# Second scores product of each head on its own 64 rows of the array, in a parallel mixer layer on one core

## The chip, the cores and the metric

The kernel runs on one core of a Trainium2 chip. The metric is the time of one execution on the device in microseconds (us). Three runs of the kernel before took 1723.13, 1725.75 and 1727.35 us; their median is 1725.75 us. The profile comes from one more execution, which took 1721.93 us, 1720.2 us of it from its first to its last instruction.

## The reference

One layer over 4096 tokens of width 1024. A projection `x @ w_in` gives the inputs of five groups of heads and a gate; the groups' outputs times `silu(gate)` go through `w_out`, and a residual with layer norm follows. The change is in the fifth group, cross-attention of each token to a memory of 256 rows, with four heads of width 64:

```
def memory_cross_attention(q, mem, w_kv):
    k, v = jnp.split(mem @ w_kv, 2, axis=-1)
    q = q.reshape(bn, s, N_SUB, HEAD_DIM)
    k = k.reshape(bn, -1, N_SUB, HEAD_DIM)
    v = v.reshape(bn, -1, N_SUB, HEAD_DIM)
    scores = jnp.einsum("bshd,bmhd->bhsm", q, k) * (1.0 / math.sqrt(HEAD_DIM))
    p = jax.nn.softmax(scores, axis=-1)
    return jnp.einsum("bhsm,bmhd->bshd", p, v).reshape(bn, s, D_G)
```

## The kernel before, in words

The tokens are worked on in four pairs of blocks of 512 (`p`). The big projection is done in 14 pairs of 128 output columns (`mpair`), by a Strassen scheme with seven products each, and every product is made of matrix products of rounded float32 parts (type float32r, one pass of TensorE), a high and a low part for both sides. These are lines L220, L222 and L223, 128 by 128 weights against 512 columns. The output projection at the end is L812.

`attention(p, i, n, src, g)` handles heads `2i` and `2i+1` (called `j` = 0 and 1) for one block of 512 tokens; it is called 16 times. `queries` makes a tile `q` of 128 rows for each head. For head 0 the rows 0 to 63 hold the rounded query and the rows 64 to 127 what the rounding left; for head 1 the halves are exchanged. The keys stand in two tiles. `k1` holds the rounded key on both halves. `k2` holds what the rounding left of the key, on the half where the rounded query stands, and zeros on the other half. So the scores of a head are two products of 128 rows each: `q` by `k1` (`r` = 0) and, on top in the same PSUM bank, `q` by `k2` (`r` = 1). In the second one 64 of the 128 rows are zeros.

Each call does this in two steps (`c2`) of two chunks of 128 tokens (`c`). In a step each head has one PSUM bank, `sc[j]`, with 256 columns for each chunk. A maximum (L622), an exponential (L626), and a division follow on VectorE and ScalarE; transposes (L639) turn the result, and L645 makes the output product. That one has weights of 64 columns only and writes the two heads to different halves of the PSUM partitions; L648 makes the two heads' products follow each other. The mixing in another group (L588) also has weights of 64 columns.

The program is written in the order of the loops, but what stands in each engine's queue is set at build time by a scheduler: it fills TensorE's queue with whatever is ready, so products of the projection, transposes and scores of an attention are mixed. All PSUM banks that are not of the projection come from one pool of four (`pa`, tag `ax`). A matrix product in the trace has two parts, the load of its weights (PEld) and the product (PE). 256 scores products are issued, 128 with `r` = 0 and 128 with `r` = 1.

Of the kernel before, what the change touches and what calls it, by code (L numbers as in the profile page):

```python
# [18 lines left out]
P = 128  # L19
# [33 lines left out]
def trunk(ctx, tc, a, out):  # L53
    nc = tc.nc
# [10 lines left out]
    def nm(s):  # L65
        uid[0] += 1
        return f"{s}_{uid[0]}"
# [5 lines left out]
    def tt(tag, dt=F32, n=None):  # L73
        cols, bufs = SLOTS[tag]
        return (wp if tag == "ws" else tp).tile([P, cols], dt, tag=tag, name=nm(n or tag), bufs=bufs)

    def const(shape, src=None, dt=F32):
        t = cp.tile(shape, dt, name=nm("c"), tag=nm("ct"))
        if src is not None:
            nc.sync.dma_start(out=t, in_=src)  # L80
        return t

    def bank(pool, tag):
        return pool.tile([P, T], F32, tag=tag, name=nm(tag))
# [151 lines left out]
    def mpair(xs):  # L236


        def step(ps, x, start, stop):
            ready(1)  # L240
            product(ps, ahead.pop(0), x, start, stop)
            ready(5)

        A = bank(pm, "mm")
        step(A, xs[PA], True, False)
        t = tt("st", n="t")
        nc.scalar.copy(out=t, in_=A)  # L247
        C = bank(pm, "mm")
        step(C, xs[PT1], True, True)
        B = bank(pm, "mm")  # L250
        step(B, xs[PT2], True, True)
        add(t, B, t)
        v = tt("st", n="v")
        add(v, C, t)
        step(A, xs[PB], False, True)
        B2 = bank(pm, "mm")
        step(B2, xs[PT3], True, False)
        c22 = tt("cc", n="cc")
        add(c22, B2, v)
        C2 = bank(pm, "mm")  # L260
        step(C2, xs[PD], True, True)
        c12 = tt("cc", n="cc")
        add(c12, C2, v)
        step(B2, xs[PT4], False, True)
        c21 = tt("cc", n="cc")
        add(c21, B2, t)
        return (A, c12), (c21, c22)
# [76 lines left out]
    k1, k2 = ([const([P, 2, 256], dt=F32R) for _ in range(2)] for _ in range(2))  # L344
# [73 lines left out]
    def store(b, k, y):  # L418
        nc.sync.dma_start(out=h[b][:, :, k], in_=y.rearrange("p (u t) -> p u t", u=2))
# [179 lines left out]
    def queries(src):  # L599

        q = tt("big", F32R, n="q")[:, :2 * T].rearrange("p (j t) -> p j t", j=2)
        for j in range(2):
            d0, d1 = 64 * j, 64 - 64 * j
            nc.scalar.copy(out=q[d0:d0 + 64, j], in_=src[d0:d0 + 64])
            nc.vector.tensor_tensor(out=q[d1:d1 + 64, j], in0=src[d0:d0 + 64], in1=q[d0:d0 + 64, j].bitcast(F32),
                                    op=ALU.subtract)
        return q

    def attention(p, i, n, src, g):
        q = queries(src)  # L610
        es = [tt("big", n="e")[:, :2 * T].rearrange("p (c m) -> p c m", c=NC4) for _ in range(2)]
        for c2 in range(2):
            sc = [bank(pa, "ax").rearrange("p (c m) -> p c m", c=2) for _ in range(2)]
            for c in range(2):
                t0 = (2 * c2 + c) * P
                for j in range(2):
                    for r, k in enumerate((k1, k2)):
                        nc.tensor.matmul(out=sc[j][:, c], lhsT=q[:, j, t0:t0 + P], rhs=k[i][:, j],  # L618
                                         start=(r == 0), stop=(r == 1))
            for j in range(2):  # L620
                mx = sp.tile([P, 2], F32, tag="mx", name=nm("mx"))
                nc.vector.tensor_reduce(out=mx, in_=sc[j], axis=AX.X, op=ALU.max, negate=True)  # L622
                e = es[j][:, 2 * c2:2 * c2 + 2]
                su = sp.tile([P, 2], F32, tag="su", name=nm("su"))
                for c in range(2):
                    nc.scalar.activation(out=e[:, c], in_=sc[j][:, c], func=AF.Exp, bias=mx[:, c:c + 1],  # L626
                                         accum_out=su[:, c:c + 1])
                ri = sp.tile([P, 2], F32, tag="ri", name=nm("ri"))
                nc.vector.reciprocal(out=ri, in_=su)
                for c in range(2):  # L630
                    nc.vector.tensor_scalar(out=e[:, c], in0=e[:, c], scalar1=ri[:, c:c + 1], scalar2=None,
                                            op0=ALU.mult)
        po = bank(pa, "ax")
        for mc in range(2):
            pTs, copies = [], []
            for j in range(2):
                pt = bank(pa, "ax")
                for c in range(NC4):
                    nc.tensor.transpose(out=pt[:, P * c:P * c + P], in_=es[j][:, c, P * mc:P * mc + P],  # L639
                                        identity=ident)  # L640
                pTs.append(tt("wk", n="pT")[:, :T])
                copies.append(nc.scalar.copy(out=pTs[j], in_=pt))  # L642
            for j in range(2):
                hd = 2 * i + j
                mm = nc.tensor.matmul(out=po[64 * j:64 * j + 64], lhsT=vm[:, mc, 64 * hd:64 * hd + 64], rhs=pTs[j],  # L645
                                      start=(mc == 0), stop=(mc == 1))
                if j == 0:
                    tc.add_manual_dep(mm.ins, copies[1].ins.name,  # L648
                                      mybir.DependencyInfo(mybir.DependencyClass.Sync, mybir.DependencyReason.DATA),
                                      reason="both heads' products follow each other")  # L650
        nc.vector.tensor_tensor(out=g, in0=po, in1=g, op=ALU.mult)
        store(2 * p + n, 8 + i, g)
# [66 lines left out]
    for p in range(NPAIR):  # L719
# [15 lines left out]
        for i in range(2):  # L735
            q, ge = mpair(xs)
            for n in range(2):
                attention(p, i, n, q[n], silu2(ge[n], ge[n]))
            mixing(p, i, vns, *mpair(xs))
# [49 lines left out]
    for b in range(NB):  # L789
        for c in range(NC4):  # L790
# [9 lines left out]
            r = [tt("cc", n="r") for _ in range(2)]  # L800
# [7 lines left out]
            for n, k in steps:  # L808
                hi, lo = hh[k]
                whi, wlo = wo[k]  # L810
                for l, ww in ((lo, whi), (hi, wlo), (hi, whi)):
                    nc.tensor.matmul(out=ps[n], lhsT=l[:, P * (c % 2):P * (c % 2) + P], rhs=ww[:, T * n:T * n + T],  # L812
                                     start=(k == 0 and l is lo), stop=(k == NKO - 1 and ww is whi and l is hi))
# [73 lines left out]
```

## Time and profile before

| what | value |
|---|---|
| median of three runs | 1725.75 us |
| profiled execution | 1721.93 us, span 1720.2 us |
| TensorE busy | 1695.2 us, 99% of the span |
| VectorE busy | 1330.6 us, 77% |
| ScalarE busy | 510.1 us, 30% |
| granted TensorE clock, mean | 0.998 |
| scores products, L618 | 256 |
| output products of attention, L645 | 128 |

A record of TensorE lasts from when a product begins to when its last result has arrived, so records of neighbours overlap. What a product costs the engine is the distance from its start to the start of the next one. In the forms "128*128 128x256" the first pair is the rows and columns of the array that the weights fill, the second the partitions and columns of the operand.

### The profile page before, as it was taken

The page shows a single profiled execution, that of the slowest core. Times are in us where ns is not written, and L with a number is a line of the kernel's source. Part 1 is how long each engine was busy: PE and PEld are TensorE (multiplying, and loading weights), DVE is VectorE, ACT ScalarE, POOL GpSimd, SP SyncE. Part 2 cuts the span into 40 slices and gives each one's busy share as a digit, 9 for nine tenths or more (in the row PEclk, how much of TensorE's full clock was granted, in tenths as well). Part 3 has the DMA queues.
Part 4 walks back from the last instruction along what each step waited for, and adds up shares of the span by engine and source line. Part 5 has one row for each costly group of instructions (what it writes and reads, how often), then busy time and mean ns, then how long its engine had stood idle before and what let it go on. Part 6 is the DMA issues. An engine that isn't in the chain of part 4 may idle for free.

```text
span 1720.2 us, 21845 instructions
## 1 busy us (share of the span) xinstructions
PE 1695.2 (99%) x7924; PEld 1370.5 (80%) x7924; DVE 1330.6 (77%) x2462; ACT 510.1 (30%) x945; POOL 50.0 (3%) x87
## 2 busy tenths in 40 slices
PE   7999999999999999999999999999999999999997
PEld 6887777878877788887778888777888888888786
DVE  8688977899966559997663999775399997555764
ACT  5334654411154332013542311354250101001200
POOL 0000000000100000010000001000000000000000
PEclk9999999999999999999999999999999999999999
DMA  8778455876744577674447767534683334332621
GB/s 278 249 310 317 184 215 224 302 243 206 236 159 147 159 258 256 210 241 163 155 138 265 247 203 230 197 130 157 222 300 123 123 119 158 119 114 74 208 76 48
DMA packets 128379, 333.83 MB, mean 194 GB/s; under 512 B 14096, under 2 KB 36112, under 8 KB 128272
## 3 DMA queue, kind: packets, MB, share of 16 engines
q1 hardware_dynamic: 128272, 332.44, 56.8%
q8 instruction: 63, 1.03, 0.2%
q14 instruction: 44, 0.36, 0.1%
HBM read 239.07 MB, written 93.32 MB: 193 GB/s over the span
## 4 chain that ended last, share of the span: by engine, by line
PE 90%; DVE 5%; DMA 2%; ACT 2%; issue 1%; SPq 0%; DVEq 0%; ACTq 0%
PE mm L812 24%; PE mm L220 19%; PE mm L223 19%; PE mm L222 19%; PE ax L645 2%; PE ax L618 2%; PE ax L639 2%; DVE xl L88 1%; DMA wq<-in_w_in 1%; PE ax L588 1%; DVE xraw L94 1%; PE ax L439 1%; ACT e L626 1%; PE ax L496 1%; PE ax L486 0%
## 5 line engine op out<-in xcount | busy, mean ns | idle before, releaser
L220 PE MATMUL mm<-xl,w 128*128 128x512 f32 x1572 | 619.1, 394 | 10.2 <-DVE xl L88 7.8
L223 PE MATMUL mm<-xh,w 128*128 128x512 f32 x1572 | 617.8, 393 | 0.0
L222 PE MATMUL mm<-xh,w 128*128 128x512 f32 x1572 | 617.6, 393 | 0.0
L812 PE MATMUL mm<-wo,h 128*128 128x512 f32 x1920 | 438.3, 390 | 1.2 <-DVE h L88 1.2
L812 PEld LDWEIGHTS mm<-wo,h 128*128 128x128 f32 x1920 | 360.0, 188 | 76.0 <-DVE h L88 1.7
L220 PEld LDWEIGHTS mm<-xl,w 128*128 128x128 f32 x1572 | 295.8, 188 | 72.0 <-DVE xl L88 7.8
L223 PEld LDWEIGHTS mm<-xh,w 128*128 128x128 f32 x1572 | 295.8, 188 | 63.8 <-issue 3.2
L222 PEld LDWEIGHTS mm<-xh,w 128*128 128x128 f32 x1572 | 296.0, 188 | 60.0 <-issue 1.0
L473 DVE SCALAR_TENSOR_TENSOR acc<-din,c,acc 128x1024 f32<-128x1024 f32 x240 | 304.2, 1280 | 0.3
L87 ACT CAST h<-hraw 128x1024 fp32r<-128x1024 f32 (+1 forms) x48 | 43.4, 911 | 309.7 <-PE mm L812 241.0
L91 DVE TENSOR_TENSOR cc<-mm,v 128x512 f32<-128x512 f32 x110 | 75.4, 688 | 58.8 <-PE mm L223 57.9
L815 DVE SCALAR_TENSOR_TENSOR r<-r,mm 128x512 f32<-128x512 f32 x64 | 43.2, 687 | 73.5 <-PE mm L812 72.2
L247 ACT COPY t<-mm 128x512 f32<-128x512 f32 x55 | 32.3, 587 | 188.0 <-PE mm L223 177.6
L399 ACT ACTIVATE cc<-cc 128x512 f32<-128x512 f32 x44 | 27.8, 633 | 154.1 <-DVE cc L91 154.0
L88 DVE TENSOR_TENSOR xl<-xraw,xh 128x1024 fp32r<-128x1024 f32 x58 | 69.0, 1222 | 5.6 <-ACT xh L87 5.5
L91 DVE TENSOR_TENSOR t<-mm,t 128x512 f32<-128x512 f32 x55 | 37.9, 689 | 44.0 <-PE mm L223 43.3
L87 ACT CAST xh<-xraw 128x1024 fp32r<-128x1024 f32 x58 | 59.2, 1050 | 42.7 <-DVE xraw L94 21.3
L88 DVE TENSOR_TENSOR h<-hraw,h 128x1024 fp32r<-128x1024 f32 (+1 forms) x48 | 49.9, 1041 | 21.8 <-ACT h L87 12.8
L626 ACT ACTIVATE e<-ax,mx 128x256 f32<-128x256 f32 x128 | 59.2, 474 | 14.1 <-DVE mx L622 13.0
L622 DVE TENSOR_REDUCE mx<-ax 128x2 f32<-128x512 f32 x64 | 42.9, 682 | 24.7 <-PE ax L618 24.4
L91 DVE TENSOR_TENSOR cc<-mm,t 128x512 f32<-128x512 f32 x55 | 37.9, 688 | 27.2 <-PE mm L223 27.0
L642 ACT COPY pT<-ax 128x512 f32<-128x512 f32 x64 | 36.1, 589 | 48.1 <-PE ax L639 47.4
(148 smaller groups left out, 1515.7 us busy)
## 6 DMA issues: line engine op xcount, KB each, us to landing
w<-wd SPq DMA_DIRECT2D x294, 512.0 KB, 4.2
wd<-w SPq DMA_DIRECT2D x98, 512.0 KB, 3.2
xraw<-in_xT SPq DMA_DIRECT2D x32, 512.0 KB, 5.0
h<-cc SPq DMA_DIRECT2D x64, 256.0 KB, 3.3
hraw<-h SPq DMA_DIRECT2D x32, 512.0 KB, 4.2
r<-in_x SPq DMA_DIRECT2D x64, 256.0 KB, 3.1
out<-r SPq DMA_DIRECT2D x64, 256.0 KB, 2.0
wraw<-in_w_in SPq DMA_DIRECT2D x24, 512.0 KB, 4.6
```

Source lines behind the costliest of these rows:

```text
L87: nc.scalar.copy(out=hi, in_=src)
L88: nc.vector.tensor_tensor(out=lo, in0=src, in1=hi.bitcast(F32), op=ALU.subtract)
L91: nc.vector.tensor_tensor(out=dst, in0=x, in1=y, op=ALU.add)
L220: nc.tensor.matmul(out=ps, lhsT=w[:, 0, k], rhs=xl[:, r], start=start and k == 0, stop=False, skip_group_check=True)
L222: nc.tensor.matmul(out=ps, lhsT=w[:, 1, k], rhs=xh[:, r], start=False, stop=False, skip_group_check=True)
L223: nc.tensor.matmul(out=ps, lhsT=w[:, 0, k], rhs=xh[:, r], start=False, stop=stop and k == 3, skip_group_check=True)
L473: nc.vector.scalar_tensor_tensor(out=accs[i], in0=dins[i][:, k:k + 2 * T], scalar=dww[:, i, k:k + 1], in1=accs[i], op0=ALU.mult, op1=ALU.add)
L622: nc.vector.tensor_reduce(out=mx, in_=sc[j], axis=AX.X, op=ALU.max, negate=True)
L626: nc.scalar.activation(out=e[:, c], in_=sc[j][:, c], func=AF.Exp, bias=mx[:, c:c + 1], accum_out=su[:, c:c + 1])
L642: copies.append(nc.scalar.copy(out=pTs[j], in_=pt))
L812: nc.tensor.matmul(out=ps[n], lhsT=l[:, P * (c % 2):P * (c % 2) + P], rhs=ww[:, T * n:T * n + T], start=(k == 0 and l is lo), stop=(k == N ...
L815: nc.vector.scalar_tensor_tensor(out=r[n], in0=r[n], scalar=ALPHA, in1=ps[n], op0=ALU.mult, op1=ALU.add)
```

## The change

The loop over `r` moves to the outside: a step first issues the four products with `k1`, of both chunks and both heads, and then the four with `k2`. The products with `k2` take only the 64 rows on which `k2` is not zero, rows 0 to 63 for head 0 and 64 to 127 for head 1. Only the first product into a bank carries the start flag. The number of matrix products and of weight loads stays 256, and each has as many columns as before. Lines behind the loop move down by one (L618 becomes L619, L645 becomes L646).

```
-            for c in range(2):
-                t0 = (2 * c2 + c) * P
-                for j in range(2):
-                    for r, k in enumerate((k1, k2)):
-                        nc.tensor.matmul(out=sc[j][:, c], lhsT=q[:, j, t0:t0 + P], rhs=k[i][:, j],
-                                         start=(r == 0), stop=(r == 1))
+            for r in range(2):
+                for c in range(2):
+                    t0 = (2 * c2 + c) * P
+                    for j in range(2):
+                        d = slice(64 * j, 64 * j + 64) if r else slice(0, P)
+                        nc.tensor.matmul(out=sc[j][:, c], lhsT=q[d, j, t0:t0 + P], rhs=(k1, k2)[r][i][d, j],
+                                         start=(r == c == 0), stop=(r == 1), skip_group_check=True)
```

How TensorE's queue changes is seen at two places. The names are those of the tiles: `c_246` and `c_247` are `k1`, `c_248` and `c_249` are `k2`, each `ax` is the PSUM bank of one head in one step.

First step of the first attention, one bank, before:

```order
L220 MATMUL mm_2051<-xl_257,w_1767 128x512
L618 MATMUL ax_1859<-c_246,q_1852 128x256
L618 MATMUL ax_1859<-c_248,q_1852 128x256
L618 MATMUL ax_1859<-c_246,q_1852 128x256
L618 MATMUL ax_1859<-c_248,q_1852 128x256
L222 MATMUL mm_2051<-xh_256,w_1767 128x512
```

The same place in the changed program:

```order
L220 MATMUL mm_2051<-xl_257,w_1767 128x512
L619 MATMUL ax_1859<-c_246,q_1852 128x256 x2
L619 MATMUL ax_1859<-c_248,q_1852 128x256 x2
L222 MATMUL mm_2051<-xh_256,w_1767 128x512
```

Here the scheduler issues one head's bank alone, so both products with `k2` are of the same head and on the same rows, and a projection product follows.

An attention of the second pair of blocks, around its output products, before (`ax_5237` and `ax_5238` are the two heads of one step, `ax_5265` is a head of the next step):

```order
L618 MATMUL ax_5237<-c_247,q_5230 128x256
L618 MATMUL ax_5237<-c_249,q_5230 128x256
L645 MATMUL ax_5192<-pT_5214,c_250 64x512
L645 MATMUL ax_5192<-pT_5221,c_250 64x512
L618 MATMUL ax_5238<-c_247,q_5230 128x256
L618 MATMUL ax_5238<-c_249,q_5230 128x256
L618 MATMUL ax_5265<-c_247,q_5230 128x256
L618 MATMUL ax_5265<-c_249,q_5230 128x256
L618 MATMUL ax_5265<-c_247,q_5230 128x256
L618 MATMUL ax_5265<-c_249,q_5230 128x256
```

The same place in the changed program:

```order
L619 MATMUL ax_5237<-c_247,q_5230 128x256 x2
L619 MATMUL ax_5238<-c_247,q_5230 128x256 x2
L619 MATMUL ax_5237<-c_249,q_5230 128x256
L619 MATMUL ax_5238<-c_249,q_5230 128x256
L646 MATMUL ax_5192<-pT_5214,c_250 64x512
L646 MATMUL ax_5192<-pT_5221,c_250 64x512
L619 MATMUL ax_5237<-c_249,q_5230 128x256
L619 MATMUL ax_5238<-c_249,q_5230 128x256
L619 MATMUL ax_5265<-c_247,q_5230 128x256 x2
L619 MATMUL ax_5265<-c_249,q_5230 128x256 x2
```

Here two pairs of different heads stand next to each other, one ahead of the output products and one behind them, and the next step's bank has its two of one head again.

## Rows read from the trace of the kernel before

**Rows 1.** Span and granted clock of the core.

```profile
core 0: 1720.2 us, clock 0.998
```

**Rows 2.** The page: busy time, share of the span, instructions; chain that ended last.

```profile
PE 1695.2 (99%) x7924; PEld 1370.5 (80%) x7924; DVE 1330.6 (77%) x2462; ACT 510.1 (30%) x945; POOL 50.0 (3%) x87
PE 90%; DVE 5%; DMA 2%; ACT 2%; issue 1%; SPq 0%; DVEq 0%; ACTq 0%
```

**Rows 3.** Busy time by stretch, here the four that hold the attentions.

```profile
185.00:280.00 95.00, 94.90 (x512) 71.50 (x511) 79.03 (x159) 57.58 (x140) 0.26 (x1) 1.00 0.50 189
505.00:590.00 85.00, 84.72 (x466) 63.72 (x466) 53.57 (x125) 43.59 (x114) 0.21 (x1) 1.00 0.45 149
815.00:900.00 85.00, 84.82 (x467) 63.89 (x466) 53.76 (x126) 43.57 (x114) 0.21 (x1) 1.00 0.44 148
1125.00:1210.00 85.00, 84.80 (x466) 63.83 (x466) 53.67 (x122) 43.58 (x115) 0.21 (x1) 1.00 0.44 147
```

**Rows 4.** Timeline of PE: start, us, engine line op, form, count; one full scores block.

```profile
242.03 0.39 PE L222 MATMUL mm<-xh,w 128*128 128x512 f32 x1
242.26 0.39 PE L223 MATMUL mm<-xh,w 128*128 128x512 f32 x1
242.49 2.08 PE L618 MATMUL ax<-c,q 128*128 128x256 f32 x16
244.40 0.40 PE L220 MATMUL mm<-xl,w 128*128 128x512 f32 x1
```

**Rows 5.** Timeline of PE around one block of L588, weights of 64 columns.

```profile
220.88 0.39 PE L222 MATMUL mm<-xh,w 128*128 128x512 f32 x1
221.10 0.39 PE L223 MATMUL mm<-xh,w 128*128 128x512 f32 x1
221.42 1.97 PE L588 MATMUL ax<-c,nrm 128*64 128x128 f32 x32
223.32 0.50 PE L220 MATMUL mm<-xl,w 128*128 128x512 f32 x1
223.66 0.40 PE L222 MATMUL mm<-xh,w 128*128 128x512 f32 x1
223.89 0.39 PE L223 MATMUL mm<-xh,w 128*128 128x512 f32 x1
```

**Rows 6.** Transposes of whole 128 by 128 tiles, timeline of PE.

```profile
214.38 1.09 PE L639 MATMUL ax<-c,e 128*128 128x128 f32 x8
215.23 0.48 PE L220 MATMUL mm<-xl,w 128*128 128x512 f32 x1
```

**Rows 7.** PE around one block of L645; its lines 2, 3: without earlier starts.

```profile
204.07 0.28 PE L618 MATMUL ax<-c,q 128*128 128x256 f32 x1
204.28 1.08 PE L645 MATMUL ax<-pT,c 128*64 128x512 f32 x4
204.28 1.07 PE L645 MATMUL ax<-pT,c 128*64 128x512 f32 x3
204.76 0.60 PE L645 MATMUL ax<-pT,c 128*64 128x512 f32 x2
205.29 0.74 PE L618 MATMUL ax<-c,q 128*128 128x256 f32 x4
205.87 0.39 PE L222 MATMUL mm<-xh,w 128*128 128x512 f32 x1
```

**Rows 8.** The block of rows 5 again, from its last two products.

```profile
223.11 0.28 PE L588 MATMUL ax<-c,nrm 128*64 128x128 f32 x2
```

**Rows 9.** Weight loads by line: duration min/median/max in ns.

```profile
L618 PEld LDWEIGHTS ax<-c,q x256: 186/189/193, 190.2 to 1187.7; 128*128 128x128 f32 x128
L645 PEld LDWEIGHTS ax<-pT,c x128: 132/134/137, 201.0 to 1197.5; 128*64 128x64 f32 x128
```

**Rows 10.** What PE's weight loads waited for, total us, times, longest.

```profile
PEld ax L645 <- ACT pT L642: 9.0, 24, 0.5
```

## The prediction

> **What bounds the kernel now.** I began with the clock, then the page, then a table by stage, then single starts on TensorE. The clock is whole nearly everywhere [rows 1], so durations are those of the higher level, 2.4 GHz. TensorE is busy for 99% of the span and makes 90% of the chain that ended last [rows 2]. That share is an average, so the four stretches with the attentions matter: TensorE is busy for 94.9 of 95.0 us in the first and about 84.8 of 85.0 in each of the others, VectorE, the next, for 79.0 and about 54 [rows 3]. There TensorE is the bound, and time that its queue gains or loses reaches the end nearly in full. The busy figure is swollen by overlapping records, so I count starts. A block of 16 scores products begins at 242.49 and the next product at 244.40: 1.91 / 16 = 0.119 us each. A projection product with 512 columns takes 0.23, from 242.26 to 242.49 [rows 4].
>
> **What the change removes.** It removes no instruction. 256 products of 256 columns and 256 weight loads stay, and a product's start-to-start time goes with its columns (0.119 for 256, 0.23 for 512 [rows 4]), not with the rows it fills. So halving the rows of 128 of them saves nothing by itself. It saves only if two products on different halves run at the same time. No row has weights of 64 rows; the nearest case is weights of 64 columns, which fill half the array the other way. There it works: L588 starts 32 products of 128 columns from 221.42 to 223.32, 0.059 each [rows 5], where transposes with as many columns and a full array take (215.23 - 214.38) / 8 = 0.106 [rows 6]. Two neighbours on different halves start together, and the pair costs one. The second starts less than 0.01 behind the first: without the first of a block of L645, the other three still begin at 204.28 [rows 7]. I take the same for halves of rows: a pair saves one product, 0.119 less some 0.006 for that distance, so 0.113.
>
> How many pairs are there? In the changed program's queue the 128 products with `k2` stand in 52 uninterrupted runs: 26 of two products of the same head (the first place shown with the change), 14 of one product of each head (the second place), and 12 of four with the heads alternating. That is 14 + 12 x 2 = 38 pairs, not 64, because the scheduler issues one bank at a time whenever a bank comes free alone. Saving: 38 x 0.113 = 4.3 us. From below it is 0, if halves of rows do not run together.
>
> **What the change adds.** Each run is a piece of half-array work between products with a full array. What such a switch costs is seen at the blocks with 64 columns.
> - Going in: L223 starts at 221.10, the first of L588 at 221.42, so 0.32 where 0.23 is usual: +0.09 [rows 5]. From scores to L645, 0.21 (204.07 to 204.28) where 0.119 is usual: +0.09 [rows 7].
> - Coming out: the last pair of L588 starts at 223.11 [rows 8], the projection at 223.32 [rows 5]. That is 0.21 for a pair that otherwise takes 2 x 0.059 = 0.12: +0.09.
> - The first product behind a switch: its weights were not loaded ahead. L220 to L222 is 0.34 (223.32 to 223.66), the next step 0.23: +0.11 [rows 5]. Four scores products behind L645 take 0.58 (205.29 to 205.87) against 4 x 0.119 = 0.476: +0.105 [rows 7].
>
> So a switch into weights of 128 columns costs 0.093 + 0.105 = 0.198 us. A switch into half the rows is not in the trace. If it behaves as the one into half the columns, the second part depends on the weight load. The two pairs of L645 start 0.48 apart (204.28, 204.76), and the load there takes 134 ns against 189 for the scores [rows 7, 9]. The half with 64 rows still has 128 columns, so I take the load of the scores and 0.198 here too. The bounds are 0 (no switch at all) and 0.198, with 0.093 between them if weights are loaded ahead across it.
>
> How many switches? A run between full-array products adds two. 15 of the 52 runs touch a block of L646, where a switch stood already, and add one. 37 x 2 + 15 = 89 switches. 89 x 0.198 = 17.6 us.
>
> The Trainium skill, TensorEngine Tiling (Array Packing), under Key Properties, has a rule against this change: changing the tiling mode, not just the tile, drains TensorE, and a mode there is a division by rows as well as by columns. The trace agrees for columns (+0.09 each way [rows 5, 7, 8]) and cannot say for rows. The same page promises up to twice the speed for 64 rows; with both, this change loses, and with the second alone it gains.
>
> **What else moves.** Other products of TensorE shift by a few places, and the number of neighbours of each kind stays the same within one; I cost that at nothing, at most 1 us either way. The maximum on VectorE and the exponential on ScalarE start some 0.2 us later in a step, hidden behind projection products; VectorE has 16 to 31 us free in each stretch [rows 3]. If that cover fails, L646 waits longer for its transposed tile, a wait that is 9.0 us in 24 places already [rows 10]. The same slack works the other way too, so of the price perhaps 1 us is absorbed; I leave it out.
>
> **Sum.** 17.6 - 4.3 = +13.3 us. On the profiled execution of 1721.93 us this is 1735.2; the median of the runs shown is 3.8 us above that execution, so the prediction is 1725.75 + 13.3 = 1739 us, 0.8% slower. Between the ends the sum goes from -4.3 (pairs, no switch) to +17.6 (switches, no pairs).
>
> **Rivals.**
> 1. Halves of rows need no switch: products of 64 rows mix freely with full ones, and pairs run together. For it: the halves of columns change which outputs are written, the halves of rows do not, so what the trace shows for columns need not hold. Against it: weights for half the array must be placed beside other weights in either case. Sum: -4.3, 1721.5 us, 0.25% faster. The two cases part at 4.3 / 89 = 0.048 us for a switch; below that the change is not slower.
> 2. A switch costs the gap only, 0.093, and the weights of the half are loaded during it. Sum: 89 x 0.093 = 8.3, less 4.3: +4.0, 1729.7 us. Against it is the +0.105 behind every switch that I looked at.
> 3. The change does not do what it says: the two halves run one after the other, because of a limit that halves of columns don't have, and the switches are paid. Sum: +17.6, 1743.4 us. For it speaks only that no row shows it working; against it, L588 and L645.
>
> **How the numbers follow.** My forecast has a chance of 0.55, rival 1 has 0.25, rival 2 has 0.12, rival 3 has 0.08. A measurement of this kernel can tell about 0.3% from no change, which is 5.2 us. The forecast and rival 3 are slower by more than that, and about a third of rival 2 with its uncertain microsecond or two: 0.55 + 0.08 + 0.04 = 0.67. Rival 1 stays inside 5.2 us unless something small comes on top, a quarter of it: 0.06 faster, and 0.27 the same. The range goes from rival 1's middle, 1721, to just short of rival 3's, 1743; about half of either rival is left out, 0.16. The forecast's own range is 1735 to 1743.
>
> **What would show it.** In the changed profile the products with `k2` should appear in a form with 64 rows. Where two of different heads are neighbours they should start some 6 ns apart; if they start 0.119 apart, rival 3 is right. From the last product with `k1` to the first with `k2` should be 0.21 us, not 0.12, and the same from the last of a run to what follows, with 0.34 instead of 0.23 behind it when that is a projection product. If these steps are 0.12 and 0.23, rival 1 is right; if only the second is normal, rival 2. The stretch of the first attentions should grow by some 3 us, a quarter of the whole, and nothing outside the attentions should change. A change in the granted clock, or a new wait of L646 worth more than 2 us, would make the prediction wrong in a way that none of these cases covers.

## The result, and the profile after

The changed kernel takes 1732.85 us (median of 5 runs, 1732.66 to 1733.77) against 1724.86 us for the kernel before (median of 5, 1723.13 to 1727.35). The ratio is 1.0053, 95% interval 1.0043 to 1.0064: slower by 0.5%. That is 8.0 us between the medians and 9 us by the ratio. The prediction was slower by 13.3 us, 1739 us, with a range of 1721 to 1743 us.

The profiled execution has a span of 1731.0 us with a granted clock of 0.999. Busy time of the engines on its page, to be read against [rows 2]:

```profile
PE 1707.3 (99%) x7924; PEld 1372.2 (79%) x7924; DVE 1331.1 (77%) x2462; ACT 509.3 (29%) x945; POOL 49.9 (3%) x87
PE 91%; DVE 5%; DMA 2%; issue 1%; ACT 1%; SPq 0%; DVEq 0%; ACTq 0%
```

Counts are the same, and TensorE is busy 12.1 us longer; VectorE and ScalarE do what they did. The groups by line of TensorE show the new form, 64 rows by 128 columns:

```profile
L619 PE MATMUL ax<-c,q 128*128 128x256 f32 x128 | 26.7, 305 | 0.0
L619 PE MATMUL ax<-c,q 64*128 64x256 f32 x128 | 24.4, 341 | 0.0
L646 PE MATMUL ax<-pT,c 128*64 128x512 f32 x128 | 34.5, 618 | 0.3
```

The timeline of TensorE at the first place shown with the change, a run of two second products of the same head (columns: start us, us, engine, line, form, count):

```profile
190.71 0.28 PE L619 MATMUL ax<-c,q 128*128 128x256 f32 x1
190.92 0.38 PE L619 MATMUL ax<-c,q 64*128 64x256 f32 x1
191.14 0.28 PE L619 MATMUL ax<-c,q 64*128 64x256 f32 x1
191.35 0.50 PE L222 MATMUL mm<-xh,w 128*128 128x512 f32 x1
191.68 0.40 PE L223 MATMUL mm<-xh,w 128*128 128x512 f32 x1
```

The steps are 0.21 into the half (0.119 without a switch [rows 4]), 0.22 to the second product, 0.21 out of it, and 0.33 from L222 to L223 (0.23 without). So a switch costs a gap of 0.09 and 0.10 for a weight load that nothing hides, in each direction. The loads show it (the same places, PEld):

```profile
191.34 0.19 PEld L222 LDWEIGHTS mm<-xh,w 128*128 128x128 f32 x1
191.45 0.19 PEld L223 LDWEIGHTS mm<-xh,w 128*128 128x128 f32 x1
191.69 0.19 PEld L220 LDWEIGHTS mm<-xl,w 128*128 128x128 f32 x1
191.92 0.19 PEld L222 LDWEIGHTS mm<-xh,w 128*128 128x128 f32 x1
```

The load of L220 begins when the product before it begins, at 191.69 and 191.68. The load of L222 behind the switch begins only at 191.34, together with its own product, and the load of L223 0.10 behind the start of the product before it. The gap of half the rows is that of half the columns, and so is the load behind the switch back to the full array [rows 5, 7].

The same view 3 us later, at a run of four with the heads alternating:

```profile
194.05 0.28 PE L619 MATMUL ax<-c,q 128*128 128x256 f32 x1
194.26 0.39 PE L619 MATMUL ax<-c,q 64*128 64x256 f32 x2
194.48 0.28 PE L619 MATMUL ax<-c,q 64*128 64x256 f32 x2
194.69 0.50 PE L222 MATMUL mm<-xh,w 128*128 128x512 f32 x1
195.03 0.40 PE L223 MATMUL mm<-xh,w 128*128 128x512 f32 x1
```

Each line with x2 holds two products that start in the same hundredth, one of each head: the pairs work. The prices of the switch are the same as above.

The first stretch of attentions, which starts within 0.4 us of where it started before, by busy time and number of products:

```profile
185.00:280.00 95.00, 94.92 (x499) 69.71 (x498) 76.35 (x156) 56.25 (x138) 0.12 (x1) 1.00 0.49 184
```

499 products begin in it instead of 512 [rows 3]. 13 of them at 0.23 are 3.0 us, near the 3.3 us per stretch that was predicted. The same is seen between the starts of two projection products that enclose the stretch, first in the kernel before, then in the changed one:

```profile
187.18 0.39 PE L220 MATMUL mm<-xl,w 128*128 128x512 f32 x1
272.97 0.39 PE L220 MATMUL mm<-xl,w 128*128 128x512 f32 x1
187.50 0.39 PE L220 MATMUL mm<-xl,w 128*128 128x512 f32 x1
276.28 0.39 PE L220 MATMUL mm<-xl,w 128*128 128x512 f32 x1
```

85.79 us have become 88.78. The other three stretches grow by 2.3, 2.7 and 2.5 us. TensorE is busy for 94.92 of the 95.00 us, as before: the switches show as distances between starts, not as idle time.

### The profile page after: what moved, and what is told of

It is laid out like the page before. It is cut to its first block, busy times and chain, and to the rows that moved or that the text cites. A ratio compares the mean times of both kernels' runs of the same rounds, so it can differ in the third digit from the quotient of the medians.

```text
span 1731.0 us, 21844 instructions
## 1 busy us (share of the span) xinstructions
PE 1707.3 (99%) x7924; PEld 1372.2 (79%) x7924; DVE 1331.1 (77%) x2462; ACT 509.3 (29%) x945; POOL 49.9 (3%) x87
## 4 chain that ended last, share of the span: by engine, by line
PE 91%; DVE 5%; DMA 2%; issue 1%; ACT 1%; SPq 0%; DVEq 0%; ACTq 0%
PE mm L813 24%; PE mm L220 19%; PE mm L222 19%; PE mm L223 19%; PE ax L619 2%; PE ax L646 2%; PE ax L640 2%; DVE xl L88 1%; PE ax L588 1%; DVE xraw L94 1%; PE ax L439 1%; PE ax L496 1%; PE ax L486 0%; DMA xraw<-in_xT 0%; PE ax L498 0%
## 5 line engine op out<-in xcount | busy, mean ns | idle before, releaser
L220 PE MATMUL mm<-xl,w 128*128 128x512 f32 x1572 | 621.8, 396 | 10.5 <-DVE xl L88 7.8
L222 PE MATMUL mm<-xh,w 128*128 128x512 f32 x1572 | 619.2, 394 | 0.0
L223 PE MATMUL mm<-xh,w 128*128 128x512 f32 x1572 | 617.7, 393 | 0.0
L220 PEld LDWEIGHTS mm<-xl,w 128*128 128x128 f32 x1572 | 295.8, 188 | 78.2 <-DVE xl L88 8.7
L222 PEld LDWEIGHTS mm<-xh,w 128*128 128x128 f32 x1572 | 295.8, 188 | 63.6 <-issue 1.8
L223 PEld LDWEIGHTS mm<-xh,w 128*128 128x128 f32 x1572 | 295.9, 188 | 60.4
L91 DVE TENSOR_TENSOR cc<-mm,v 128x512 f32<-128x512 f32 x110 | 75.1, 686 | 58.1 <-PE mm L223 57.4
L91 DVE TENSOR_TENSOR t<-mm,t 128x512 f32<-128x512 f32 x55 | 37.8, 688 | 47.2 <-PE mm L223 46.3
L91 DVE TENSOR_TENSOR cc<-mm,t 128x512 f32<-128x512 f32 x55 | 37.8, 688 | 28.1 <-PE mm L223 27.9
L446 ACT ACTIVATE nrm<-ax,nmr,rs 128x256 f32<-128x256 f32 x64 | 30.5, 568 | 60.7 <-DVE nmr L444 60.7
```

The source lines that it names most:

```text
L91: nc.vector.tensor_tensor(out=dst, in0=x, in1=y, op=ALU.add)
L220: nc.tensor.matmul(out=ps, lhsT=w[:, 0, k], rhs=xl[:, r], start=start and k == 0, stop=False, skip_group_check=True)
L222: nc.tensor.matmul(out=ps, lhsT=w[:, 1, k], rhs=xh[:, r], start=False, stop=False, skip_group_check=True)
L223: nc.tensor.matmul(out=ps, lhsT=w[:, 0, k], rhs=xh[:, r], start=False, stop=stop and k == 3, skip_group_check=True)
```

## The experiments

Two theories stood against each other. Switch theory: what costs is the 89 switches between work on the full and on half the array, and 38 pairs give a part back. Order theory: what costs is the new order of the queue. A third one says that a halved product costs a fixed amount, whatever stands beside it. All ratios are to the kernel before on the same chip.

**The new order, all rows.**

```
-                        d = slice(64 * j, 64 * j + 64) if r else slice(0, P)
+                        d = slice(0, P)
```

> The new order of the loops, but both products on all 128 rows; TensorE's queue has the same sequence as in the changed kernel, with 52 runs of second products. Switch theory (the 89 added switches between full-array and half-array work cost the time, the 38 pairs give some back): no switch, no pair, so the kernel stands where the kernel before stands, within 2 us, and every step between scores products is about 0.12 us. Order theory (what costs is the new order: a head's bank is finished later, transposes and projection products interleave otherwise): this kernel is some 8 to 9 us slower than before, like the changed one.

Measured: 1722.24 us against 1723.82; ratio 0.9990 (0.9981 to 1.0000). The order theory falls: alone, the new order costs nothing and may gain 1 to 2 us. TensorE's queue has the same sequence as in the changed kernel, product by product.

**Both heads on the same half.**

```
-                        d = slice(64 * j, 64 * j + 64) if r else slice(0, P)
+                        d = slice(0, 64) if r else slice(0, P)
```

> The changed kernel with both heads' second products on rows 0 to 63, in the same sequence of TensorE's queue; the correction by the rounded-off part of the key is left out for heads 1 and 3 (their rows 0 to 63 of that key tile are zeros), so only the time counts. Switch theory: the switches stay, the 38 pairs no longer run together; a pair's second product starts some 0.22 us behind the first in runs of one pair and 0.12 inside runs of four, and the kernel is 38 x 0.116 = 4.4 us slower than the changed one, some 13 us slower than before. Theory that halves cost by themselves, pairs or not: the same time as the changed kernel.

Measured: 1736.61 us; ratio 1.0070 (1.0054 to 1.0085), 12.8 us by the medians and some 4 above the changed kernel. The number of switches is the same, and no two halves start together any more. The timeline of TensorE at the run of four:

```profile
194.80 0.73 PE L619 MATMUL ax<-c,q 64*128 64x256 f32 x4
195.46 0.50 PE L222 MATMUL mm<-xh,w 128*128 128x512 f32 x1
```

Four products take 0.66 until the next one starts, where the changed kernel has 0.43 (194.26 to 194.69). The difference, 0.23, is two products: what the pairs are worth. The switch is paid either way.

**Every second product in a pair.** Each second product waits for the last first product of the other head.

```
+                        if r == 0:
+                            whole.append(mm)
+                        else:
+                            tc.add_manual_dep(mm.ins, whole[3 - j].ins.name, ...)
```

> The changed kernel with a dependence that lets the second products start only when the first products of both heads are issued, so every one of them has the other head's beside it: 24 runs of four and 16 of two at blocks of output products, 64 pairs, 64 added switches. Switch theory: 64 x 0.198 - 64 x 0.116 = +5.3 us against before, some 6 us less than the changed kernel by the same sum (12.8 to 13.3), give or take 2 us of waits for PSUM banks. Theory that halves cost by themselves: no change against the changed kernel. If pairs are what counts and switches are cheap: faster than before.

Measured: 1725.94 us against 1723.82; ratio 1.0014 (1.0003 to 1.0025), +2.4 us (0.5 to 4.3). The direction and the order of size hold: 25 fewer switches and 26 more pairs take back some 6 to 7 us of the changed kernel's 8 to 9. The sum of +5.3 lies above the interval. If this order gains by itself what the order of the first experiment does, 1 to 2 us, it is 3.3 to 4.3, inside the interval at its upper edge; this order with all rows was not run.

**Halves in the old order.** The kernel before with rows `d` in its second products.

```
-                        nc.tensor.matmul(out=sc[j][:, c], lhsT=q[:, j, t0:t0 + P], rhs=k[i][:, j], ...)
+                        d = slice(64 * j, 64 * j + 64) if r else slice(0, P)
+                        nc.tensor.matmul(out=sc[j][:, c], lhsT=q[d, j, t0:t0 + P], rhs=k[i][d, j], ...)
```

> The order of the kernel before, but the second product of each chunk and head on its 64 rows: 128 runs of a single second product, no pair, 248 added switches. Switch theory: 248 x 0.198 = +49 us, some 1774 us; from a first product to the second 0.21 us, from the second to the next product 0.31 with the load of its weights exposed, and 0.22 to 0.34 behind that. Theory that each halved product costs a fixed amount (9 us over 128, 0.07 each): +9 us, as the changed kernel without its pairs at most +14.

Measured: 1779.03 us; ratio 1.0318 (1.0300 to 1.0336), +55 us. The theory of a fixed cost falls: the same 128 halved products cost some six times as much when each stands alone. The timeline of TensorE in the first step:

```profile
190.78 0.38 PE L619 MATMUL ax<-c,q 64*128 64x256 f32 x1
191.09 0.39 PE L619 MATMUL ax<-c,q 128*128 128x256 f32 x1
191.40 0.38 PE L619 MATMUL ax<-c,q 64*128 64x256 f32 x1
191.72 0.50 PE L222 MATMUL mm<-xh,w 128*128 128x512 f32 x1
```

Every step is 0.31 to 0.32 instead of 0.119: two switches for each half. The time is 6 us above the sum of 49, and the trace shows something that no theory named, the clock. Busy time and granted clock (the third number from the end of each row) around the first block of 12 scores products:

```profile
193.20:196.20 3.00, 3.00 (x11) 1.66 (x9) 1.33 (x2) 2.04 (x8) 0.00 (x0) 1.00 0.19 78
196.20:203.00 6.80, 6.80 (x17) 5.05 (x17) 5.43 (x16) 2.54 (x10) 0.00 (x0) 0.50 0.24 80
203.00:206.00 3.00, 3.00 (x18) 2.28 (x17) 0.00 (x0) 0.73 (x2) 0.00 (x0) 1.00 0.00 0
```

The clock is whole up to 196.20, in a block where whole and half products alternate, then at its lower level for 6.8 us, and the products behind the block pay. The timeline of TensorE there:

```profile
198.26 0.63 PE L220 MATMUL mm<-xl,w 128*128 128x512 f32 x1
198.69 0.63 PE L222 MATMUL mm<-xh,w 128*128 128x512 f32 x1
```

A projection product takes 0.43 instead of 0.23. The profile has six such stretches in the attentions, 27.3 us in all. In them 45 steps from one projection product to the next take 0.44 on average, 9.5 us more than at 0.23. The span is 57.2 us over that of before, 8 more than the sum, so the clock is enough to account for the 8; how much a switch costs at the lower clock was not separated.

**Both steps of an attention joined, and the same order with all rows.** Four banks are taken at once; eight first products, then eight second ones in a fixed order. The second kernel has `d = slice(0, P)`.

```
+        scs = [[bank(pa, "ax").rearrange("p (c m) -> p c m", c=2) for _ in range(2)] for _ in range(2)]
+        for r in range(2):
+            for t in range(NC4):
+                for j in range(2):
+                    d = slice(64 * j, 64 * j + 64) if r else slice(0, P)
+                    mm = nc.tensor.matmul(out=scs[t // 2][j][:, t % 2], lhsT=q[d, j, t * P:t * P + P],
+                                          rhs=(k1, k2)[r][i][d, j], ...)
+                    whole.append(mm)
+                    if r:
+                        tc.add_manual_dep(mm.ins, whole[-2].ins.name, ...)
```

> The changed kernel with both steps of an attention joined: four PSUM banks at once, the eight first products, then the eight second products in a fixed order with the heads alternating. 16 runs of second products instead of 52, 64 pairs, 32 added switches. Switch theory: 32 x 0.198 - 64 x 0.116 = -1.1 us against the same order with all rows (the next kernel); the pairs just pay for the switches. Inside a run the starts come 3 ns and 0.12 us apart in turn. Theory that halved products cost by themselves: some 9 us slower than the next kernel, as the changed kernel is against its own order with all rows.

> The same order as the joined kernel, with all 128 rows in every product: no switch and no pair. It holds all four banks of the pool at a time, so output products and transposes may wait for a bank: 0 to +6 us against before. It is the base for the joined kernel, which should stand 1 us below it by the switch theory.

Measured: joined 1722.21 us, ratio 0.9999 (0.9990 to 1.0008); with all rows 1721.33 us, ratio 0.9986 (0.9977 to 0.9995). So the halves do not cost 9 us here, and they do not gain either: by the medians the joined kernel stands 0.9 us above its base where 1.1 below was expected, and the two intervals overlap. Timeline of TensorE, joined kernel, a run of eight:

```profile
193.28 0.74 PE L618 MATMUL ax<-c,q 64*128 64x256 f32 x8
193.95 0.50 PE L223 MATMUL mm<-xh,w 128*128 128x512 f32 x1
```

Eight products in 0.67, where eight whole ones take 8 x 0.119 = 0.95. Add the gap of 0.09 before it and the load of 0.11 behind it, and 0.87 remains: 0.08 gained by a run, 1.3 us by 16 of them. At the scores themselves the sum holds. The gain is lost elsewhere, in the steps around the transposes (below).

**The changed kernel and its order with all rows, side by side.** No new edit.

> The changed kernel once more, beside its own order with all rows on the same chip, to size what the halves alone do. By the steps of its trace: 89 switches at 0.193 less 38 pairs at 0.116, +12.8 us against the next kernel, and some 9 to 11 us against before. If halves and order share the time otherwise, the two stand less than 10 us apart.

> The new order with all rows, again: 0 to 3 us faster than before, 10.5 to 13 us faster than the changed kernel.

Measured: 1732.29 us, ratio 1.0059 (1.0045 to 1.0072), and 1721.64 us, ratio 0.9995 (0.9987 to 1.0004). The halves alone cost 10.7 us by the medians. Spans and clocks of the two profiles, the changed kernel first:

```profile
core 0: 1732.6 us, clock 0.999
```

```profile
core 0: 1719.8 us, clock 0.999
```

The distance is 12.8 us here, the sum of the steps, but that is partly chance: the profiled run of the changed kernel took 1734.34 us, 2 us above the median of its five, and that of the other kernel stood at its median. A group by line of the order with all rows shows the scores products as they were before the change:

```profile
L619 PE MATMUL ax<-c,q 128*128 128x256 f32 x256 | 40.1, 292 | 0.0
```

**The four stretches alone.** Whole runs of the kernel before differ by up to 8.6 us from each other, which hides effects of 1 us. The traces can be compared without that: from one start of L220 ahead of a stretch of attentions to one behind it (the 226th and 311th of the 1572 products of L220, the 631st and 701st, the 1023rd and 1093rd, the 1415th and 1485th), summed over the four stretches and less the same in the kernel before:

| kernel | us against before |
|---|---|
| changed kernel, its two profiles | +10.4, +10.5 |
| new order, all rows, its two profiles | -1.3, -1.3 |
| both heads on the same half | +14.7 |
| every second product in a pair | +2.8 |
| halves in the old order | +56.1 |
| joined, and joined with all rows | -0.6, -1.5 |

The pairs are worth 14.7 - 10.4 = 4.3 us, against 4.4 expected. The halves cost 10.5 + 1.3 = 11.8 against the same order with all rows: the steps at the scores and between projection products grow by 12.6, close to the 12.8 by the sum of steps, and the steps into, between and out of the transposes shrink by 0.8. In the joined kernels the halves cost 0.9: 1.2 is gained at the scores and behind them, as expected, and 2.0 is lost in the steps around the transposes (L648). Why the transposes move, and why the new order gains 1.3, stays open.

## Why the prediction was right

- **TensorE is the bound in the attentions.** Right. The four stretches grew by 10.4 us and the span by 10.8; no engine's idle time took the added time up.
- **A switch into or out of half the rows costs 0.198 us, as one into weights of 128 columns did before.** Right, and this was the doubtful step. Measured: 0.09 in, 0.09 out, 0.10 for the load behind each, 0.193 together. Rival 2 (the gap only) is excluded by the 0.22 and 0.33 behind the switches, rival 1 (no switch) by the gaps of 0.09 and by the fourth experiment. The rule of the Trainium skill (TensorEngine Tiling (Array Packing), Key Properties) is that a change of the tiling mode drains TensorE. The trace agrees for rows as well, with +0.09 at each switch.
- **Two halves side by side cost one.** Right: they start in the same hundredth, and without that the kernel is some 4 us slower (second experiment; 4.4 expected). Rival 3 is excluded. The step from columns to rows was a guess that held. The rows that the pair was read from, L588 and L645, are plain float32, not float32r as the scores, and there a product takes nearly twice as long for the same columns. In the kernel before two of them with 256 columns take 0.43:

```profile
31.29 0.60 PE L358 MATMUL ax<-memT,wkv 128*128 128x256 f32 x2
31.72 0.59 PE L360 MATMUL ax<-wkv,memT 128*128 128x256 f32 x2
```

  The pair of L645 with 512 columns takes 0.53 less the gap of 0.09 = 0.44 [rows 7]. That looks like two products at 0.23, but it is the price of one product of its type, 2 x 0.215 = 0.43. So the reading of the pair stands, and the rule that the time goes with the columns holds only within one type. The Trainium skill (TensorEngine Tiling (Array Packing), Theoretical Speedup) gives up to twice the speed for a dimension of at most 64. The trace agrees for a pair, and not for the kernel.
- **38 pairs and 89 switches.** Right: the queue ran in the order in which it was built, and the trace has the 52 runs.
- **The sum.** Mis-sized, 13.3 against 8 to 11. The measured 1732.85 us lies below the 1735 to 1743 that the prediction gave as the forecast's own range, and the added time lies midway between the forecast and rival 2, so the number alone does not choose between them; the steps do. With the measured prices the sum is 89 x 0.193 - 38 x 0.116 = 12.8. The term that failed is "what else moves, at nothing": in the four stretches the new order alone gains 1.3 us and the steps around the transposes 0.8 more, 2.1 together where the prediction allowed 1 us either way; 10.4 is what the stretches grew by. The new order measures 0.9 us (-2.2 to +0.7) and 1.7 us (-3.3 to 0) below the kernel before as a whole, in line with the 1.3. The rest, some 1 to 2.4 us between 10.4 and the medians, is within the scatter of the kernel before, whose single runs went from 1720.28 to 1728.89 us. Its base of 1725.75 was a median of three runs, 2 us above the medians of 15 to 23 runs that later stood beside the experiments.

## What to carry to other kernels

A product on half the array was not cheaper by itself here; only a pair saved, one product's start-to-start time. Count the switches in the queue as it is built, not in the loops: here a switch cost 0.19 us and a pair of 256 columns saved 0.116, so a stay in the half has to hold four pairs before it pays at all. The scheduler decided what stands side by side and made 38 pairs of 64; forcing the order gave all 64. Even then the best of these versions had no halves in it (0.14% under the kernel before, interval 0.05% to 0.23%).

## What the runs showed of the hardware that was not expected

In the kernel with single halves between full products (fourth experiment) the granted clock fell from 1.00 to 0.50 though TensorE had work all the time: six times in the attentions, twice for 6.8 us and four times for 3.4, each time in or behind a block where whole and half products alternate. All four of its runs show it, with a mean clock of 0.989 to 0.991 against 0.996 to 0.999 in the kernel before. In the changed kernel, with 52 runs in place of 128, the clock stays at 1.00 in the same stretches. That the halves as such do it was not separated from the switches.

The clock also fell in two kernels outside the attentions, in the profiles of the first and the second experiment. There TensorE had waited 1.9 us for VectorE (L91) shortly before. In the first experiment, the product behind the wait and then busy time and clock:

```profile
350.72 0.50 PE L220 MATMUL mm<-xl,w 128*128 128x512 f32 x1 [1.93 <-DVE t L91]
```

```profile
352.20:355.60 3.40, 3.40 (x9) 2.64 (x8) 2.62 (x4) 0.00 (x0) 0.00 (x0) 0.50 0.77 296
```

Both were the slowest runs of their kernels, 3.5 and 2.5 us above the median, so such a stretch is probably one part of the scatter. Of 59 runs of the kernel before, the 11 with a mean clock of 0.997 or less have a median of 1725.8 us and the others 1722.8.

Halves of rows start closer together than halves of columns do: in the trace of the changed kernel the two products of a pair of L646 are 6 to 7 ns apart, those of a pair of L619 2 to 4 ns.
